# Linear attention's stages given out two slices later, and the modulations' sums ordered behind the scores' last step on VectorE

## The chip, the cores and the metric

The kernel runs on one core of one Trainium2 chip. The metric is the device time of one launch, in microseconds (us). The kernel before took 630.38 us, the median of three runs (629.6, 630.38, 630.89). Smaller is better.

## The reference

It is one layer of a diffusion backbone: 256 latent tokens (with 256 context tokens beside them) of width 1024, modulated by a conditioning vector, mixed by three branches in parallel, merged, and sent through a mixture of 16 experts. Cut to what the change touches:

```
shift1, scale1, gate1, shift2, scale2, gate2 = split(silu(c) @ w_mod + b_mod, 6)
h = modulate(rms_norm(x), shift1, scale1)
proj = h @ w_in                       # keys, values, decays, queries, gates, branch gates
# linear attention (gla), chunks of 64 tokens, forwards and backwards:
q_dec = q * exp(cum); k_inv = k * exp(-cum)
att = where(mask, q_dec @ k_inv.T, 0)            # "scores"
o = att @ v + q_dec @ state                      # "values", and the part carried by the states
y_gla = rms_norm(o) * silu(out_gate)             # "normed"
m = sum(sigmoid(gate_b) * (y_b @ w_b) for b in (hyena, gla, attention))
x = x + gate1 * (m @ w_out)
x = x + gate2 * moe(modulate(rms_norm(x), shift2, scale2))
```

The vectors `scale2` and `shift2` (`sc2`, `sh2` in the kernel) are products of one vector with a 1024x1024 weight each, and are needed only by the experts' stage.

## The kernel before

Everything is one function, `tile_backbone_layer`. The weights of the projections come from memory as float32 tiles (`wf`, 1 MB each) on SyncE's DMA queue. ScalarE casts half a tile at a time to its high part (`whi`, L281) and VectorE subtracts to get its low part (`wlo`, L282); TensorE then does three products for each piece, high by high, high by low and low by high (`proj_tok`, L689 to L691, into banks `pj`; `proj_col`, L699 to L701, into banks `pc`). Both `whi` and `wlo` have three buffers each.

A quarter of such a tile is a *slice*, and `weight_slice` hands slices out in turn. They are numbered by `nslice`; the ones that matter here are 16 to 23 (output gates of linear attention, `og`), 24 to 31 and 32 to 39 (attention queries, `aq0`, `aq1`) and 40 to 47 (first branch gate, `br0`). Piece names carry the tile's place: `wlo_aq010` is the low part of half 0, tile 1, first two slices of `aq0` (its names begin aq0); `wlo_010` belongs to the first branch gate.

Behind the matmuls of each slice `slice_done` gives out whatever two lists, `stages` and `mods`, hold for that slice's number. Giving out means that the instructions are written into the program there; a scheduler with a cost model of its own then settles the order on each engine. `tc.issue_after(last_mm[0])` adds an order, on TensorE alone, behind the last matmul of the slice. VectorE's instructions from `mods` have no such order: the scheduler puts them where its model has room.

The stages of linear attention come for two halves of the tokens, t = 0 and 1:

- `gla_scores(t)`: the part carried by the states (L1065, banks `go`) and the scores (L1087, banks `ga`) on TensorE, then on VectorE two predicated copies that apply the mask (L1090) and an addition of the two directions (L1091), all in the tile `aka`.
- `gla_values(t)`: TensorE adds the scores' part to `go` (L1099); ScalarE squares; VectorE scales the sums of squares (`sg`, L1105) and GpSimd raises them to the power -0.5 (L233).
- `gla_normed(t)`: VectorE refines the root (L240 to L242) and scales and gates the outputs (`yg`, L1113, four instructions).
- `gla_transpose(t)`: TensorE transposes (`ygT`), ScalarE and VectorE split into two parts (L1122, L1123).

Other stages between them are the rotary turn of the queries (`rp_q`, L1145 to L1149), their transposes (`qTp`, `kTp` for the keys, all L275) and the powers for their norms (`qv`, L1210, on GpSimd again L233).

The modulations' sums are vector work: `mod_load` (L365) brings a quarter of a weight column block, 1 MB (`wm`), and two `mod_macc` add its two rows of 1024 to a running sum on VectorE (L377, `macc<-wm*csg+macc`). The sum of `sc2` has its own tile; that of `sh2` lies in the tile `gt`. `mod_sums` then sums over the partitions on TensorE (L290, `mc_sc`, `mc_sh`). Quarter 3 of `sc2` (`wm_sc23`) and quarter 1 of `sh2` (`wm_sh21`) use one after the other the same slot of memory, number 14, and the attention queries' tile `qT` takes that slot next. The list gives out these maccs at slices 27 to 30 and 40.

Of the kernel before, what the change touches and what calls it, by code (L numbers as in the profile page):

```python
# [16 lines left out]
ALU = mybir.AluOpType  # L17
# [138 lines left out]
def tile_backbone_layer(ctx: ExitStack, tc: tile.TileContext, I: dict, out: bass.AP):  # L156
    nc = tc.nc
    V, S, T, G, SP = nc.vector, nc.scalar, nc.tensor, nc.gpsimd, nc.sync
# [24 lines left out]
    def slot(i, shape, nm, dtype=F32):  # L183
        return big.tile(shape, dtype, tag=f"s{i}", bufs=1, name=nm)
# [32 lines left out]
    def mbank(nm):  # L217
        return psM.tile([P, 512], F32, tag="mm", name=nm)
# [402 lines left out]
    for k4 in range(4):  # L621
# [4 lines left out]
                    op=ALU.add)  # L626
# [38 lines left out]
                modulated(0, step)  # L665


    stages, mods, nslice, last_mm = {}, {}, [-16], [None]

    def slice_done():  # L670

        with tc.issue_after(last_mm[0]):
            for f, *a in stages.pop(nslice[0], []) + mods.pop(nslice[0], []):
                f(*a)
        nslice[0] += 1

    def proj_tok(n, nm, streams, hook=None):
# [47 lines left out]
    for u in (2, 0, 1):  # L725
# [4 lines left out]
        for i in range(4):  # L730
            blk = u * 4 + i
            src = bk[i // 2][:, (i % 2) * NT:(i % 2 + 1) * NT]
            a = uc[u][:, i, :]
# [145 lines left out]
    for s, f, *a in ((None, hyena_time, 0),  # L879
# [20 lines left out]
        else:  # L900
            stages.setdefault(s, []).append((f, *a))
    bk = proj_tok(512, "kv1", (0, 1), slice_done)
    for r in range(2):
        for t in range(2):
            S.copy(gk[:, r, t, :], bk[r, t][:, 0:256])
            S.copy(gv[:, r, t, 0:256], bk[r, t][:, 256:512])
    bk = proj_tok(288, "kv2", (0, 1), slice_done)
    for r in range(2):
        for t in range(2):
# [142 lines left out]
    am, ygla = [], []  # L1052
# [3 lines left out]
    def gla_carried(t):  # L1056


        ob = obs[t] = [mbank(f"go{t}{hb}").rearrange("p (c v) -> p c v", c=4)[:, 0:2, :] for hb in range(2)]
        for cb in range(2):  # L1060
            for dr in range(2):
                for cp in range(2):
                    n = 2 * t + cp
                    for hb, hs in enumerate(half):
                        T.matmul(ob[hb][64 * cp:64 * cp + 64, cb, :], lhsT=qd[dr][hs, cb, n * 64:(n + 1) * 64],  # L1065
                                 rhs=St[hs, n, dr, cb, :], start=(cb == 0 and dr == 0), stop=False,
                                 skip_group_check=True)

    def gla_scores(t):
        gla_carried(t)  # L1070
        if t == 0:

            am.append(aka[:, 0:768].rearrange("p (d h c q) -> p d h c q", d=3, h=2, c=2))
            G.memset(am[0][:, 0:2], 0.0)

            am.append(gg[0][:, 512:640].rearrange("p (d q) -> p d q", d=2))
            for c in range(2):
                cs = slice(64 * c, 64 * c + 64)
                G.tensor_copy(am[1][cs], trg[cs, 0:2, cs])
            ygla.append(slot(15, [P, 2, 4, NT], "ygla", F32R))  # L1080
        ab = [mbank(f"ga{t}{hb}")[:, 0:256].rearrange("p (d c q) -> p d c q", d=2, c=2) for hb in range(2)]
        for dr in range(2):
            for cb in range(2):
                for cp in range(2):
                    n = slice(64 * (2 * t + cp), 64 * (2 * t + cp) + 64)
                    for hb, hs in enumerate(half):
                        T.matmul(ab[hb][64 * cp:64 * cp + 64, dr, cb, :], lhsT=ki[dr][hs, cb, n], rhs=qd[dr][hs, cb, n],  # L1087
                                 start=True, stop=True, skip_group_check=True)
        for hb in range(2):
            V.copy_predicated(am[0][:, 0:2, hb], am[1][:, :, None, :].bitcast(U32).to_broadcast([P, 2, 2, 64]), ab[hb])  # L1090
        V.tensor_tensor(am[0][:, 2], am[0][:, 0], am[0][:, 1], op=ALU.add)  # L1091

    def gla_values(t):
        ob = obs[t]
# [140 lines left out]
    for s, f in ((0, (decay_weights,)),  # L1235
                (0, (decay_inputs,)),
                (1, (decay_exp, 0)),
                (1, (decay_exp, 1)),
                (1, (decay_exp, 2)),
                (1, (decay_exp, 3)),  # L1240
                (5, (decay_log,)),
                (6, (context_keys, 0)),
                (7, (context_keys, 1)),
                (8, (decayed_keys, 0)),
                (8, (context_state,)),
                (9, (end_keys, 0)),
                (9, (end_keys, 1)),
                (10, (decayed_keys, 1)),
                (11, (key_norms,)),
                (13, (rope_tables,)),  # L1250
                (13, (key_rope, 0)),
                (14, (chunk_states, (0, 1))),
                (16, (key_rope, 1)),
                (17, (chunk_states, (3, 2))),
                (18, (key_transpose, 0)),
                (19, (key_rope, 2)),
                (19, (key_transpose, 1)),
                (21, (gla_scores, 0)),
                (23, (key_rope, 3)),
                (24, (gla_values, 0)),  # L1260
                (24, (key_transpose, 3)),
                (26, (gla_scores, 1)),
                (26, (gla_normed, 0)),
                (28, (gla_transpose, 0)),
                (27, (key_transpose, 2)),
                (30, (gla_values, 1)),
                (32, (gla_normed, 1)),
                (34, (gla_transpose, 1)),
                (33, (query_transpose, 0, 1)),
                (36, (query_transpose, 0, 0)),  # L1270
                (43, (query_transpose, 1, 0)),
                (43, (query_transpose, 1, 1))):
        stages.setdefault(s, []).append(f)
    aka = slot(16, [P, 2048], "aka")
    ak = aka[:, 1024:2048].rearrange("p (i d) -> p i d", i=4)
    av = slot(9, [P, 2, 4, 256], "av", F32R)
    bk = proj_tok(512, "kv0", (0, 1), slice_done)
    for r in range(2):
        for t in range(2):
# [680 lines left out]
```

## Time and profile before

| | before |
|---|---|
| median of 3 runs | 630.38 us |
| the profiled execution's own time | 629.4 us |
| its span in the trace | 627.6 us |
| TensorE busy | 598.1 us (95%) |
| VectorE busy | 363.2 us (58%) |
| ScalarE busy | 263.1 us (42%) |
| GpSimd busy | 34.0 us (5%) |
| mean granted clock of TensorE | 0.991 |

The span runs from the first to the last instruction; the execution's time has 1.8 us around it. The profiled execution was 0.98 us under the median. Linear attention's later stages and the attention queries lie between 180 and 260 us; the experts' stage, limited by TensorE, starts at about 408 us. Times in the views are us from the start of the span. "Idle before" an instruction is the time in which its engine did nothing just ahead of it, with what ended that.

### The profile page before, as it was taken

The numbers are of one execution on the slowest core, as the hardware profiler recorded it, in microseconds if no ns is written. First come the engines' busy times: TensorE is split into PE (matmuls) and PEld (weight loads), VectorE is DVE, ScalarE is ACT, GpSimd is POOL, SyncE is SP. The second block draws the span as 40 slices with busy tenths as digits, with TensorE's granted clock in tenths as the row PEclk, the third lists the DMA queues.
The fourth block names the chain that finished last, engine by engine and source line by source line (L and its number), as shares of the span: only waits on it lengthen the run. The fifth ranks groups of instructions, "written<-read, shape, count | busy, mean of one in ns | idle before, by whom it ended". The sixth has DMA issues, their size and how long they took to land.

```text
span 627.6 us, 9837 instructions
## 1 busy us (share of the span) xinstructions
PE 598.1 (95%) x3907; PEld 424.6 (68%) x3907; DVE 363.2 (58%) x675; ACT 263.1 (42%) x485; POOL 34.0 (5%) x37
## 2 busy tenths in 40 slices
PE   4799999999998999999999999899999999999994
PEld 2339878788886789899999999653534434343332
DVE  6779979597588898979974485430412303212122
ACT  4747851447754667655634444430302202111012
POOL 1200400030100210000000000000000000000000
PEclk9999999999999999999999999989999999999997
DMA  8997722155655446795998689989999999999992
GB/s 259 390 346 251 235 71 68 67 168 181 256 202 174 175 142 225 266 324 181 386 350 308 240 291 324 333 301 338 410 409 409 409 409 409 408 410 409 409 388 86
DMA packets 60701, 179.12 MB, mean 285 GB/s; under 512 B 4644, under 2 KB 7396, under 8 KB 59368
## 3 DMA queue, kind: packets, MB, share of 16 engines
q1 hardware_dynamic: 60288, 177.66, 76.2%
q8 instruction: 33, 0.54, 0.3%
q0 software_dynamic: 192, 0.47, 0.2%
q10 hardware_dynamic: 168, 0.29, 0.1%
q14 instruction: 20, 0.16, 0.1%
HBM read 177.35 MB, written 1.05 MB: 284 GB/s over the span
## 4 chain that ended last, share of the span: by engine, by line
PE 82%; DVE 8%; DMA 4%; ACT 3%; issue 1%; POOL 1%; SPq 0%; ACTq 0%; POOLq 0%
PE gug L270 9%; PE guu L270 9%; PE y L270 9%; PE pc_br L699 4%; PE pc_br L701 4%; PE pc_br L700 4%; PE accm L270 3%; PE hgm L270 3%; PE pj_kv L689 2%; PE pj_kv L691 2%; PE pj_kv L690 2%; PE pc_hy L700 2%; PE pc_hy L701 2%; DMA wm_sh<-in_w_mod_dram 2%; PE pc_hy L699 2%; PE yb L1331 2%
## 5 line engine op out<-in xcount | busy, mean ns | idle before, releaser
L270 PE MATMUL gug<-mg,hgm 128*64 128x512 f32 x256 | 59.6, 597 | 0.0
L1802 DVE SCALAR_TENSOR_TENSOR y<-y,gsl,gt 128x256 f32<-128x256 f32 x32 | 15.0, 488 | 76.7 <-PE y L270 73.8
L270 PE MATMUL guu<-mu,hgm 128*64 128x512 f32 x256 | 56.7, 595 | 0.0
L270 PE MATMUL y<-md,hT 128*64 128x512 f32 x256 | 56.6, 593 | 0.0
L699 PE MATMUL pc_br<-hThi,whi 128*128 128x256 f32 x192 | 55.5, 289 | 0.0
L701 PE MATMUL pc_br<-hThi,wlo 128*128 128x256 f32 x192 | 54.3, 284 | 0.0
L700 PE MATMUL pc_br<-hTlo,whi 128*128 128x256 f32 x192 | 54.2, 282 | 0.0
L270 PEld LDWEIGHTS y<-md,hT 128*64 128x64 f32 x256 | 18.2, 137 | 36.1 <-issue 31.4
L281 ACT CAST wkm<-y 128x256 fp32r<-128x256 f32 x32 | 11.9, 373 | 72.1 <-DVE y L1802 71.5
L270 PEld LDWEIGHTS guu<-mu,hgm 128*64 128x64 f32 x256 | 17.7, 137 | 33.1 <-issue 30.3
L270 PEld LDWEIGHTS gug<-mg,hgm 128*64 128x64 f32 x256 | 17.6, 138 | 32.5 <-issue 31.8
L699 PEld LDWEIGHTS pc_br<-hThi,whi 128*128 128x128 f32 x192 | 36.6, 191 | 1.4 <-issue 0.8
L700 PEld LDWEIGHTS pc_br<-hTlo,whi 128*128 128x128 f32 x192 | 36.7, 191 | 0.5
L689 PE MATMUL pj_kv<-whi_kv,hThi 128*128 128x512 f32 (+1 forms) x96 | 36.6, 381 | 0.0
L701 PEld LDWEIGHTS pc_br<-hThi,wlo 128*128 128x128 f32 x192 | 36.6, 191 | 0.0
L281 ACT CAST whi<-wf 128x1024 fp32r<-128x1024 f32 x24 | 25.2, 1050 | 24.8 <-PE pc_br L700 13.1
L690 PE MATMUL pj_kv<-wlo_kv,hThi 128*128 128x512 f32 (+1 forms) x96 | 34.7, 362 | 0.0
L691 PE MATMUL pj_kv<-whi_kv,hTlo 128*128 128x512 f32 (+1 forms) x96 | 34.5, 360 | 0.0
L282 DVE TENSOR_TENSOR wlo<-wf,whi 128x1024 fp32r<-128x1024 f32 x24 | 29.2, 1218 | 9.0 <-ACT whi L281 9.0
L1879 ACT COPY hT<-hp 128x512 f32<-128x512 f32 x8 | 4.7, 586 | 71.0 <-PE hp L275 71.0
L1865 DVE TENSOR_TENSOR sg<-sg,guu 128x512 f32<-128x512 f32 x8 | 5.5, 687 | 48.7 <-PE guu L270 48.7
L700 PE MATMUL pc_hy<-hTlo,whi_hy 128*128 128x256 f32 x96 | 27.3, 287 | 0.5 <-DVE hTlo L656 0.5
(459 smaller groups left out, 1495.3 us busy)
## 6 DMA issues: line engine op xcount, KB each, us to landing
mg<-in_moe_w_gate_dram SPq DMA_DIRECT2D x64, 512.0 KB, 10.2
mu<-in_moe_w_up_dram SPq DMA_DIRECT2D x64, 512.0 KB, 10.2
md<-in_moe_w_down_dram SPq DMA_DIRECT2D x62, 512.0 KB, 10.2
wf<-in_w_in_dram SPq DMA_DIRECT2D x12, 1024.0 KB, 7.9
wm<-in_w_mod_dram SPq DMA_DIRECT2D x7, 1024.0 KB, 12.0
wf_hy<-in_w_in_dram SPq DMA_DIRECT2D x5, 1024.0 KB, 8.9
wf_kv<-in_w_in_dram SPq DMA_DIRECT2D x4, 1024.0 KB, 5.1
wm_sc<-in_w_mod_dram SPq DMA_DIRECT2D x4, 1024.0 KB, 6.1
```

The lines of the kernel that those rows point to most:

```text
L270: m = f(*a, **kw)
L281: S.copy(hi, src)
L282: last_lo[0] = V.tensor_tensor(lo, src, hi.bitcast(F32), op=ALU.subtract).ins
L689: T.matmul(o, lhsT=hi[:, k, tk], rhs=whi, start=(k == 0), stop=False)
L690: T.matmul(o, lhsT=hi[:, k, tk], rhs=wlo, start=False, stop=False)
L691: last_mm[0] = T.matmul(o, lhsT=lo[:, k, tk], rhs=whi, start=False, stop=(k == 7)).ins
L699: T.matmul(o, lhsT=hi, rhs=mv[0], start=(first and i % 2 == 0), stop=False, skip_group_check=True)
L700: T.matmul(o, lhsT=hi, rhs=mv[1], start=False, stop=False, skip_group_check=True)
L701: return T.matmul(o, lhsT=lo, rhs=mv[0], start=False, stop=last, skip_group_check=True)
L1331: T.matmul(yb[:, (h % 2) * NT:(h % 2 + 1) * NT], lhsT=av[:, i, n, kvh * P:(kvh + 1) * P], rhs=p[:, n, :], start=(n == m == 0), stop=(n == ...
L1802: V.scalar_tensor_tensor(yf, yf, gsl, gt2[:, c * 512 + f:c * 512 + f + 256], op0=ALU.mult, op1=ALU.mult)
L1865: V.tensor_tensor(sg.rearrange("s (j p) -> s j p", j=4), sg.rearrange("s (j p) -> s j p", j=4), ub.rearrange("s (p j) -> s j p", j=4), op= ...
```

## The change

Three edits. `slice_done` gives out the stages first and the modulations' instructions behind them, these under a second order: behind the instruction that `stage_dve` holds, if there is one. `gla_scores` puts its last VectorE instruction, the addition, into `stage_dve`, so every modulation instruction that is given out after a scores stage stands behind that stage's addition on VectorE. And the table moves most of linear attention's stages one or two slices later.

```
     def slice_done():
         with tc.issue_after(last_mm[0]):
-            for f, *a in stages.pop(nslice[0], []) + mods.pop(nslice[0], []):
+            for f, *a in stages.pop(nslice[0], []):
                 f(*a)
+
+            with tc.issue_after(stage_dve[0]) if stage_dve[0] else ExitStack():
+                for f, *a in mods.pop(nslice[0], []):
+                    f(*a)
         nslice[0] += 1
...
-        V.tensor_tensor(am[0][:, 2], am[0][:, 0], am[0][:, 1], op=ALU.add)
+        stage_dve[0] = V.tensor_tensor(am[0][:, 2], am[0][:, 0], am[0][:, 1], op=ALU.add).ins
...
-                (24, (gla_values, 0)),
+                (25, (gla_values, 0)),
...
-                (26, (gla_scores, 1)),
-                (26, (gla_normed, 0)),
-                (28, (gla_transpose, 0)),
+                (27, (gla_normed, 0)),
+                (29, (gla_transpose, 0)),
                 (27, (key_transpose, 2)),
-                (30, (gla_values, 1)),
+                (28, (gla_scores, 1)),
+                (32, (gla_values, 1)),
...
```

`gla_normed(1)` and `gla_transpose(1)` go from 32 and 34 to 34 and 36. Behind the new lines all line numbers are 4 higher.

The first place is VectorE at the scores of the first half. Here `ga00` and `ga01` are that half's scores, `aka` the tile that the addition closes, `gt2` the sum of `sh2`; the first piece is the kernel before, the second the changed one.

```order
239 L377 SCALAR_TENSOR_TENSOR gt2_71<-wm_sh20_1984,csg_67,gt2_71 128x1024
240 L282 TENSOR_TENSOR wlo_aq001_1866<-wf_aq00_1804,whi_aq001_1865 128x1024
241 L1090 COPY_PREDICATED aka_1350<-gg_1712,ga00_1838 128x2x128
242 L1090 COPY_PREDICATED aka_1350<-gg_1712,ga01_1839 128x2x128
243 L377 SCALAR_TENSOR_TENSOR gt2_71<-wm_sh21_2053,csg_67,gt2_71 128x1024
244 L1091 TENSOR_TENSOR aka_1350<-aka_1350 128x256
245 L377 SCALAR_TENSOR_TENSOR gt2_71<-wm_sh21_2053,csg_67,gt2_71 128x1024
```

```order
237 L282 TENSOR_TENSOR wlo_aq001_1866<-wf_aq00_1804,whi_aq001_1865 128x1024
238 L1094 COPY_PREDICATED aka_1350<-gg_1712,ga00_1838 128x2x128
239 L1094 COPY_PREDICATED aka_1350<-gg_1712,ga01_1839 128x2x128
240 L1095 TENSOR_TENSOR aka_1350<-aka_1350 128x256
241 L1237 SCALAR_TENSOR_TENSOR gg_1712<-th0_1879,pj_og00_1716 128x512
242 L1237 SCALAR_TENSOR_TENSOR gg_1712<-th1_1882,pj_og01_1717 128x512
```

Three sums of `sh2` stood before, between and behind the three steps of the scores; now the low part of a weight, the two copies and the addition follow each other.

The second place is VectorE at the scores of the second half (`ga10`, `ga11`), before and changed; `kT` is the keys' transposed tile and `ygla` the split output of the first half.

```order
258 L282 TENSOR_TENSOR wlo_aq011_1987<-wf_aq01_1915,whi_aq011_1986 128x1024
259 L1090 COPY_PREDICATED aka_1350<-gg_1712,ga10_1953 128x2x128
260 L1090 COPY_PREDICATED aka_1350<-gg_1712,ga11_1954 128x2x128
261 L1091 TENSOR_TENSOR aka_1350<-aka_1350 128x256
262 L282 TENSOR_TENSOR wlo_aq100_2019<-wf_aq10_2016,whi_aq100_2018 128x1024
263 L282 TENSOR_TENSOR kT_1348<-kTp2_1996,kT_1348 128x2x128
264 L1123 SCALAR_TENSOR_TENSOR ygla_1837<-ygT0_2008,pk_65,ygla_1837 128x4x128
265 L282 TENSOR_TENSOR wlo_aq101_2062<-wf_aq10_2016,whi_aq101_2061 128x1024
266 L377 SCALAR_TENSOR_TENSOR gt2_71<-wm_sh22_2057,csg_67,gt2_71 128x1024
```

```order
254 L282 TENSOR_TENSOR wlo_aq100_2012<-wf_aq10_2009,whi_aq100_2011 128x1024
255 L282 TENSOR_TENSOR kT_1348<-kTp2_1957,kT_1348 128x2x128
256 L1094 COPY_PREDICATED aka_1350<-gg_1712,ga10_1987 128x2x128
257 L1094 COPY_PREDICATED aka_1350<-gg_1712,ga11_1988 128x2x128
258 L1095 TENSOR_TENSOR aka_1350<-aka_1350 128x256
259 L377 SCALAR_TENSOR_TENSOR macc_sc2_1213<-wm_sc23_1927,csg_67,macc_sc2_1213 128x1024
260 L377 SCALAR_TENSOR_TENSOR gt2_71<-wm_sh20_1935,csg_67,gt2_71 128x1024
261 L1127 SCALAR_TENSOR_TENSOR ygla_1837<-ygT0_2021,pk_65,ygla_1837 128x4x128
262 L377 SCALAR_TENSOR_TENSOR macc_sc2_1213<-wm_sc23_1927,csg_67,macc_sc2_1213 128x1024
263 L282 TENSOR_TENSOR wlo_aq101_2045<-wf_aq10_2009,whi_aq101_2044 128x1024
```

The low part `wlo_aq100` and the keys' copy now stand ahead of the scores' steps, and behind the addition come the two sums of `sc23`, which stood some sixty rows earlier (rows 199 and 201 of the kernel before), and the first sum of `sh20` (row 239 before). The rest of `sh2` follows in the changed program at rows 276 to 301, two each of `sh21`, `sh22` and `sh23`; the other product of `sh20`, the first of its sum, is ScalarE's (L375) in both kernels.

The third place is TensorE in the first branch gate, at the first use of the low part with number 2282 (`wlo_010`), before and changed; 2448 and 2449 are the banks of the same gate's second half.

```order
1046 L701 MATMUL pc_br_2262<-hThi_377,wlo_2200 128x256
1047 L275 MATMUL qTp_2337<-tri,rp_q_2233 128x128 x4
1048 L699 MATMUL pc_br_2261<-hThi_377,whi_2281 128x256
1049 L700 MATMUL pc_br_2261<-hTlo_378,whi_2281 128x256
1050 L699 MATMUL pc_br_2262<-hThi_377,whi_2281 128x256
1051 L700 MATMUL pc_br_2262<-hTlo_378,whi_2281 128x256
1052 L701 MATMUL pc_br_2261<-hThi_377,wlo_2282 128x256
1053 L699 MATMUL pc_br_2261<-hThi_377,whi_2281 128x256
```

```order
1051 L703 MATMUL pc_br_2262<-hThi_377,whi_2281 128x256
1052 L704 MATMUL pc_br_2262<-hTlo_378,whi_2281 128x256
1053 L703 MATMUL pc_br_2448<-hThi_377,whi_2377 128x256
1054 L704 MATMUL pc_br_2448<-hTlo_378,whi_2377 128x256
1055 L703 MATMUL pc_br_2449<-hThi_377,whi_2377 128x256
1056 L704 MATMUL pc_br_2449<-hTlo_378,whi_2377 128x256
1057 L275 MATMUL qTp_2337<-tri,rp_q_2233 128x128 x4
1058 L705 MATMUL pc_br_2261<-hThi_377,wlo_2282 128x256
```

Four matmuls of the gate's second half, which need only a high part, now stand ahead of the first matmul on `wlo_010`.

On TensorE the scores of the second half now come 12 projection matmuls and one transpose of keys later, its values from the last part of `aq0` into the first of `aq1`, and the eight column sums of `sh2` (L290) stand together, where before attention's products split them into five and three. On GpSimd the power of the first queries (`qv`, 128x8) now stands ahead of that of the second half's `sg` (128x4). On SyncE's queue the load of `wm_sh21` moves from behind the first tile of `aq0` to behind the first tile of the branch gate, seven issues later.

## Rows read from the trace of the kernel before

**Rows 1.** the profile page, part 1: busy us of each engine

```profile
PE 598.1 (95%) x3907; PEld 424.6 (68%) x3907; DVE 363.2 (58%) x675; ACT 263.1 (42%) x485; POOL 34.0 (5%) x37
```

**Rows 2.** waits of TensorE: line waited for, total us, times, longest us

```profile
PE go L1099 <- DVE aka L1091: 1.0, 1, 1.0
...
PE ga L1087 <- DVE yg L1113: 0.9, 1, 0.9
...
PE qTp L275 <- DVE rs_y L242: 0.5, 1, 0.5
```

**Rows 3.** VectorE's timeline: start us, us, engine, line, operation, tiles

```profile
191.46 1.27 DVE L377 SCALAR_TENSOR_TENSOR gt<-wm_sh,csg,gt 128x1024 f32<-128x1024 f32 x1
192.65 0.41 DVE L1091 TENSOR_TENSOR aka<-aka 128x256 f32<-128x256 f32 x1
```

**Rows 4.** TensorE's timeline, 194 to 200 us; idle before, and its releaser, in brackets

```profile
194.39 0.47 PE L689 MATMUL pj_aq<-whi_aq,hThi 128*128 128x512 f32 x1
...
197.33 1.10 PE L1065 MATMUL go<-St,qd 64*64 64x128 f32 x32
199.31 0.95 PE L1087 MATMUL ga<-qd,EK 64*64 64x64 f32 x32 [0.87 <-DVE yg L1113]
```

**Rows 5.** VectorE's timeline, 197 to 231 us

```profile
197.79 0.16 DVE L240 TENSOR_TENSOR rs_t<-rs_y 128x4 f32<-128x4 f32 x1 [0.80 <-POOL rs_y L233]
...
200.56 0.77 DVE L1090 COPY_PREDICATED aka<-gg,ga 128x256 f32<-128x256 uint32 x2
201.36 0.42 DVE L1091 TENSOR_TENSOR aka<-aka 128x256 f32<-128x256 f32 x1
...
204.12 0.41 DVE L282 TENSOR_TENSOR kT<-kTp,kT 128x256 fp32r<-128x256 f32 x1
...
229.46 1.22 DVE L282 TENSOR_TENSOR wlo<-wf,whi 128x1024 fp32r<-128x1024 f32 x1
```

**Rows 6.** one stretch by engine: us; busy (instructions); clock, DMA share, GB/s

```profile
201.78:230.67 28.89, 28.35 (x183) 23.50 (x181) 24.83 (x48) 19.57 (x59) 5.08 (x3) 1.00 0.52 182
```

**Rows 7.** TensorE's timeline at the column sums and at wlo_010's first use

```profile
222.25 1.10 PE L290 MATMUL mc_sc<-macc_sc,tri 128*32 128x128 f32 x16
...
231.06 0.28 PE L700 MATMUL pc_br<-hTlo,whi 128*128 128x256 f32 x1
231.18 0.28 PE L701 MATMUL pc_br<-hThi,wlo 128*128 128x256 f32 x1
...
255.38 1.07 PE L290 MATMUL mc_sh<-gt,tri 128*32 128x128 f32 x10
...
257.88 0.63 PE L290 MATMUL mc_sh<-gt,tri 128*32 128x128 f32 x6
```

**Rows 8.** GpSimd's timeline: the powers

```profile
196.75 1.01 POOL L233 TENSOR_TENSOR rs_y<-sg,mhalf 128x4 f32<-128x4 f32 x1 [26.25 <-DVE sg L1105]
209.78 2.03 POOL L233 TENSOR_TENSOR rs_y<-sg,mhalf 128x4 f32<-128x4 f32 x1 [12.02 <-DVE sg L1105]
215.46 2.08 POOL L233 TENSOR_TENSOR rs_y<-qv,mhalf 128x8 f32<-128x8 f32 x1 [3.65 <-DVE rs_t L241]
229.69 3.08 POOL L233 TENSOR_TENSOR rs_y<-qv,mhalf 128x8 f32<-128x8 f32 x1 [12.15 <-DVE qv L1210]
```

**Rows 9.** line L365 on SyncE's queue: times from issue to landing

```profile
DMA to landing us min/median/max: 4.7/6.1/8.1
```

**Rows 10.** TensorE's timeline ahead of the experts

```profile
406.19 0.38 PE L1691 MATMUL rk<-mask,tri 128*128 128x32 f32 x2 [2.23 <-DVE mask L1683]
...
407.61 0.69 PE L270 MATMUL hgm<-Om,x1hi 128*128 128x256 f32 x2 [0.83 <-DVE Om L1732]
```

**Rows 11.** stretches of 2 us behind it, columns as in group 6

```profile
408.00:410.00 2.00, 1.91 (x9) 1.70 (x10) 1.77 (x3) 0.00 (x0) 0.00 (x0) 0.61 1.00 373
410.00:412.00 2.00, 2.00 (x10) 1.66 (x11) 0.97 (x3) 0.87 (x2) 0.00 (x0) 0.53 0.99 397
412.00:414.00 2.00, 2.00 (x11) 0.71 (x8) 1.31 (x6) 0.57 (x3) 0.00 (x0) 1.00 0.17 61
```

More of the change, by code (lines that the diff above doesn't have):

```diff
@@ L665, in tile_backbone_layer @@
                 modulated(0, step)
-    stages, mods, nslice, last_mm = {}, {}, [-16], [None]
+    stages, mods, nslice, last_mm, stage_dve = {}, {}, [-16], [None], [None]
     def slice_done():
         with tc.issue_after(last_mm[0]):
-            for f, *a in stages.pop(nslice[0], []) + mods.pop(nslice[0], []):
+            for f, *a in stages.pop(nslice[0], []):
                 f(*a)
+            with tc.issue_after(stage_dve[0]) if stage_dve[0] else ExitStack():
+                for f, *a in mods.pop(nslice[0], []):
+                    f(*a)
         nslice[0] += 1
@@ L1259, in tile_backbone_layer @@
                 (23, (key_rope, 3)),
-                (24, (gla_values, 0)),
+                (25, (gla_values, 0)),
                 (24, (key_transpose, 3)),
-                (26, (gla_scores, 1)),
-                (26, (gla_normed, 0)),
-                (28, (gla_transpose, 0)),
+                (27, (gla_normed, 0)),
+                (29, (gla_transpose, 0)),
                 (27, (key_transpose, 2)),
-                (30, (gla_values, 1)),
-                (32, (gla_normed, 1)),
-                (34, (gla_transpose, 1)),
+                (28, (gla_scores, 1)),
+                (32, (gla_values, 1)),
+                (34, (gla_normed, 1)),
+                (36, (gla_transpose, 1)),
                 (33, (query_transpose, 0, 1)),
```

## The prediction

> **What bounds the kernel now.** I read the page first, then TensorE's waits, then the timelines of the two engines between 190 and 260 us, last the stretches. The page has TensorE busy for 598.1 us of the span of 627.6 [rows 1], so a gain can only come from the rest, or from matmuls that follow each other better. TensorE's waits show how much of that rest linear attention holds: its values wait 1.0 for VectorE's addition of the scores, its second scores 0.9 for the gated outputs `yg`, and one transpose of queries 0.5 [rows 2]. That is 2.4 us, and it is all that the change can take away there. Of the first wait 1.2 is a sum of `sh2`, which stands between the predicated copies and the addition: it starts at 191.46, the addition at 192.65 [rows 3]. But VectorE, at 58% over the span [rows 1], isn't loose here: between the end of the second addition and the end of `wlo_010`, a stretch of 28.89 us, it is busy for 24.83 [rows 6]. It has 4.06 us to give in that stretch.
>
> **What the change removes.** All three waits. For the first half the addition follows the copies directly, and TensorE has six projection matmuls and a transpose ahead of the values. The second scores come 12 matmuls later on TensorE, a good 2.9 us (194.39 to 197.33 [rows 4]), against a wait of 0.87 there. The third wait ended behind the same crowded VectorE; its transposes now come later. Sum: -2.4 us of waits, if nothing else is late.
>
> **What it moves.** The sums cost VectorE as much as before, 1.19 each (191.46 to 192.65 [rows 3]); only their place is new. Behind the second addition stand nine of them up to `wlo_010`, where four stood: two of `sc23`, one of `sh20` and two of `sh21` have come in. I follow VectorE to that point.
>
> - Start. The second `ga` ended at 199.31 + 0.95 = 200.26 [rows 4]. It loses the two waits ahead of it (1.0 + 0.87 = 1.86, unrounded) and gets the 12 matmuls with the switch to them (2.94): 201.34. Copies and addition take from 200.56 to 201.36 + 0.42 = 201.78 [rows 5], that is 1.22. So the addition ends at 202.6, against 201.78.
> - Work. 24.83 [rows 6] plus 5 x 1.19 = 5.95, less `wlo_aq100` and the keys' copy, which now stand ahead of the addition (1.2 as `wlo_010`, and 0.41 [rows 5]; 1.6 together): 29.2 us.
> - Idle. Of 4.06 before, nearly all goes, since the extra sums fill the time in which VectorE was ahead of the others. It can't be under 0. From above I take 0.7, the one gap of the kind that ended on a slower engine in rows here (0.80 <- GpSimd [rows 5]), less what the extra work hides; I use 0.35.
> - End of `wlo_010`: 202.6 + 29.2 + 0.35 = 232.15.
>
> TensorE first used `wlo_010` at 231.18, half a microsecond after it was there (229.46 + 1.22 = 230.68 [rows 5, 7]): it did not wait. Now it arrives, without its 2.4 of waits and with four matmuls ahead at 0.12 each (231.06 to 231.18 [rows 7]; 0.48), at 231.18 - 2.4 + 0.48 = 229.26, and waits until 232.15: about 2.9 us. The stalls removed are collected again at one place. What is left of the sum: 232.15 - 231.18 = +1.0 at that matmul, -0.48 for the four matmuls that are done by then.
>
> Behind it I add one gain: the column sums of `sh2` stood in two pieces, 1.07 and 0.63, and stand in one now, as those of `sc2` did in 1.10 [rows 7]. The difference is 0.6; since the last matmul of each piece overlaps what follows, I take 0.5. Other groups on TensorE (`ygT`, `qTp`) also get new neighbours; the same 0.6, either way, bounds them, and I take 0.
>
> Sum: +1.0 - 0.5 - 0.5 = 0.0 us.
>
> **What I cost at nothing.** The first half's `gla_normed` and `gla_transpose`, one slice later each: their readers are branch products far behind. The later end of `sc2`'s sum: its column sums stand at 222.25 [rows 7], and `sc23`'s second sum ends four VectorE instructions of at most 1.2 behind 202.6, by 207.4. That end also frees slot 14, and only then can `wm_sh21` be issued. It lands 4.7, 6.1 or 8.1 us later (least, median, most [rows 9]): 212.1, 213.5 or 215.5. VectorE reaches its first sum of `sh21` thirteen instructions later: three `wlo` at 1.2 and eight of the rotary turn, between the keys' copy's 0.41 [rows 5] for half their number and some 0.7 for those of double width (an estimate from it), so 7 to 8 us, 214.4 to 215.4. At the median the cover is 1 us; at the worst landing 1 us is lost. SyncE's queue holds other loads behind that issue, the branch gate's third and later tiles; they are wanted more than 10 us later.
>
> GpSimd's two powers change places: the one for `qv` now runs first, and the gated outputs of the second half need the other. From `qv`'s scaling to the first reader of `sg`'s power VectorE has two `wlo`, a sum, a last rotary step and a scaling, 4.2 us with the above durations; the two powers took 2.08 and 2.03 [rows 8], so 4.1. The cover is just enough. A power has also taken 1.01 and 3.08 [rows 8]. One at 3.08 costs 1.0, two cost 2.0, and as VectorE has no idle time left there, TensorE pays it. Bounds 0 and 2.0, and I take 0, by the two rows that are nearest in place.
>
> **The rivals.**
>
> *Faster: the waits go for good.* VectorE would have to have `wlo_010` when TensorE comes, at 229.26. Then -2.4 - 0.5 = -2.9: 627.5 against the median. For it: only one of nine sums is wanted soon. Against: the order on VectorE is fixed, and 29.2 us of work behind 202.6 can't end before 231.8. What I can see is a part of it: no idle (-0.35), scores some 0.3 sooner, neighbours that help (-0.6), about -1.3: 629.1.
>
> *Slower: the clock.* The collected wait of 2.9 us at one place costs more than itself if TensorE's clock falls. Ahead of the experts it was idle for 2.23, did a few small matmuls, and was idle again for 0.83 [rows 10]; the granted clock then showed 0.61 and 0.53 for 2 us each, and 1.00 again [rows 11]; behind linear attention's waits of 1.0 and 0.9 it was 1.00 [rows 2, 6]. The loss would be 2 x 0.39 + 2 x 0.47 = 1.7 us: 632.1. It decides from a wait about as long as that 2.23; against it, matmuls on high parts break mine up.
> [...]
>
> *Slower: GpSimd.* Its power took 1.01 where VectorE stood idle for 0.80 until it ended, and 2.03 to 3.08 in the stretch where VectorE had work [rows 5, 8]. In the changed kernel VectorE has no gap there, and two powers stand one behind the other: 1.0 to 2.0 us, 631.4 to 632.4.
> [...]
>
> *The change does less than it says* would be a scores' step that is still interrupted; the order on VectorE excludes it.
>
> **How the numbers follow.** The profiled execution took 629.4 us (span 627.6 and 1.8 around it), 0.98 under the median. With 0.0 the own time stays 629.4 and the median 630.4. What a measurement tells from no change is 0.2%, 1.26 us. Chances: the sum as worked out, with costs at their middle, 0.58; the gain, in part or whole, 0.16; the clock 0.13; GpSimd 0.13. Half of the last lies over 631.6, and a twentieth of the first goes there by a late `wm_sh21` or new neighbours; so slower 0.13 + 0.07 + 0.04 = 0.24, faster 0.16, same 0.60. The likeliest case's own range is 629.4 to 631.5 (idle 0 to 0.7, neighbours 0.6 either way, load 0 to 1). The range reaches to the clock's 632.1 above, and to the partial gain's 629.1 and a little below: 628.8 to 632.2.
>
> **What would show it.** In the changed profile: no wait of the values for the addition, nor of `ga` for `yg`; VectorE without gaps from about 202 to 232, over 98% busy; a new wait of TensorE for `wlo` (L282) of 2 to 3 us in the first branch gate, near 230; two sums of `sc` behind 202 us, and `wm_sh21` issued near 207. A clock under 1.00 between 228 and 236 is the second rival; a gap on VectorE ended by GpSimd the third. I am wrong if the wait for `wlo_010` is under 1 us, or if new waits stand in other places than the branch gate.

## The result: 0.5% slower

The changed kernel takes 632.77 us (median of 7 runs) against 630.16 (7 runs); the ratio is 1.0052, 95% interval 1.0032 to 1.0072. In a second comparison it was 631.99 against 629.40, ratio 1.0036, 1.0017 to 1.0055. (A ratio and its interval are estimated from all runs and need not be the quotient of the medians.) The predicted 630.4 was wrong, and the time lies above its range; so does 1.0036 of the 630.38 that it started from, 632.7. What the second rival said would happen did: behind TensorE's new wait of 1.70 us its granted clock was 0.50 in a stretch of 2 us.

The profiled execution took 632.19 us (span 630.3). It ran 0.7 us ahead of the one of before until the first scores, so I compare a stretch that both share: from the first half's carried scores to attention's last product. These are its first and last row on TensorE, of before:

```profile
186.25 1.10 PE L1065 MATMUL go<-St,qd 64*64 64x128 f32 x32
...
324.44 0.28 PE L1331 MATMUL yb<-pThi,av 128*128 128x256 f32 x1
```

and of the changed kernel:

```profile
185.54 1.10 PE L1069 MATMUL go<-St,qd 64*64 64x128 f32 x32
...
327.35 0.28 PE L1335 MATMUL yb<-pThi,av 128*128 128x256 f32 x1
```

The stretch has grown from 138.19 to 141.81, by 3.6 us; everything behind it takes the same time within 0.3. TensorE's waits in the changed kernel (line waited for, total, times, longest):

```profile
PE rk L1695 <- DVE mask L1687: 2.2, 1, 2.2
PE pc_br L705 <- DVE wlo L282: 2.2, 2, 1.7
...
PE mc_sh2c L296 <- ACT mc_sh2r L293: 0.9, 1, 0.9
...
PE pc_br L703 <- ACT whi L281: 0.5, 1, 0.5
```

The three waits of [rows 2] are gone; no line of them is left. In their place stand 2.2 for `wlo` (0.46 at `wlo_001`, 1.70 at `wlo_010`), 0.54 for the high part in between, 0.94 at the second step of `sh2`'s column sums, and 0.10 at the second `ga`. Together 3.74 for 2.40: waits alone make +1.3. Of the other 2.3 the clock makes 1.7, as the next rows show. The wait of 0.54 ended on ScalarE's cast of the high part, which had itself waited for TensorE's matmuls on an older one:

```profile
228.34 1.05 ACT L281 CAST whi<-wf 128x1024 fp32r<-128x1024 f32 x1 [1.05 <-PE pc_br L704]
```

The stretches around the new waits, with the columns of [rows 6]:

```profile
228.00:230.00 2.00, 1.46 (x11) 1.06 (x9) 1.67 (x3) 1.62 (x3) 0.00 (x0) 1.00 0.00 0
230.00:232.00 2.00, 0.88 (x6) 0.64 (x6) 2.00 (x5) 1.66 (x9) 0.47 (x1) 1.00 0.00 0
232.00:234.00 2.00, 1.43 (x9) 1.43 (x10) 2.00 (x4) 0.00 (x0) 2.00 (x1) 0.80 0.00 0
234.00:236.00 2.00, 2.00 (x8) 1.80 (x7) 2.00 (x4) 1.42 (x3) 0.01 (x1) 0.50 0.09 20
236.00:238.00 2.00, 2.00 (x16) 1.91 (x15) 1.87 (x4) 0.17 (x1) 0.00 (x0) 0.85 0.92 297
```

TensorE is busy for 1.46 and 0.88 of two stretches of 2 us, and behind them the granted clock is 0.80, 0.50 and 0.85, where it was 1.00 before. That is 2 x (0.20 + 0.50 + 0.15) = 1.7 us of clock. Its timeline shows what that does:

```profile
229.45 0.39 PE L703 MATMUL pc_br<-hThi,whi 128*128 128x256 f32 x1 [0.54 <-ACT whi L281]
...
230.28 0.60 PE L275 MATMUL qTp<-tri,rp_q 128*128 128x128 f32 x4
232.57 0.39 PE L705 MATMUL pc_br<-hThi,wlo 128*128 128x256 f32 x1 [1.70 <-DVE wlo L282]
...
233.31 1.05 PE L275 MATMUL qTp<-tri,rp_q 128*128 128x128 f32 x4
...
234.81 1.48 PE L1307 MATMUL sc<-kT,qT 128*128 128x512 f32 x3
...
255.61 0.86 PE L1307 MATMUL sc<-kT,qT 128*128 128x512 f32 x3
```

Four transposes took 0.60 at 230.28 and 1.05 at 233.31, and three score products 1.48 at 234.81; three such products took 0.86 at 255.61, where the clock was 1.00. Another 0.35 stand ahead of the fall, at a clock of 1.00: behind the wait of 0.54 four matmuls took 0.83 from start to start (229.45 to 230.28), at 0.12 each as in [rows 7] it would be 0.48. No row here says why.

VectorE does nearly what was worked out. Its rows from the second addition on, and the stretch up to the end of `wlo_010`:

```profile
201.46 0.42 DVE L1095 TENSOR_TENSOR aka<-aka 128x256 f32<-128x256 f32 x1
201.80 1.28 DVE L377 SCALAR_TENSOR_TENSOR macc_sc<-wm_sc,csg,macc_sc 128x1024 f32<-128x1024 f32 x1
...
213.64 1.32 DVE L377 SCALAR_TENSOR_TENSOR gt<-wm_sh,csg,gt 128x1024 f32<-128x1024 f32 x1 [0.20 <-DMA wm_sh<-in_w_mod_dram]
...
224.80 0.75 DVE L1127 SCALAR_TENSOR_TENSOR ygla<-ygT,pk,ygla 128x512 fp32r<-128x512 f32 x1 [0.70 <-ACT ygla L1126]
...
229.91 0.69 DVE L1149 TENSOR_TENSOR rp_q<-qs,ropet 128x512 f32<-128x512 f32 x1 [0.33 <-ACT qs L1199]
...
231.30 1.22 DVE L282 TENSOR_TENSOR wlo<-wf,whi 128x1024 fp32r<-128x1024 f32 x1
```

```profile
201.80:232.52 30.72, 28.08 (x177) 22.80 (x175) 29.36 (x51) 19.65 (x58) 5.11 (x3) 1.00 0.58 205
```

The addition ends at 201.88 (in before's times 0.7 later, 202.6; predicted 202.6), and the next instruction starts at 201.80. VectorE is busy for 29.36 us (predicted 29.2) of 30.72. The idle time is 1.36, where I took 0.35: 0.70 and 0.33 for ScalarE, 0.20 for the load of `wm_sh21`.

### The profile page after: what moved, and what is told of

Same layout as the page of the kernel before. It is cut to its first block, busy times and chain, and to the rows that moved or that the text cites. A ratio compares the mean times of both kernels' runs of the same rounds, so it can differ in the third digit from the quotient of the medians.

```text
span 630.3 us, 9835 instructions
## 1 busy us (share of the span) xinstructions
PE 599.3 (95%) x3907; PEld 426.6 (68%) x3907; DVE 363.2 (58%) x675; ACT 263.0 (42%) x485; POOL 33.6 (5%) x37
## 3 DMA queue, kind: packets, MB, share of 16 engines
HBM read 177.35 MB, written 1.05 MB: 283 GB/s over the span
## 4 chain that ended last, share of the span: by engine, by line
PE 78%; DVE 8%; DMA 6%; ACT 5%; issue 1%; POOL 1%; SPq 0%; ACTq 0%; DVEq 0%
PE gug L270 9%; PE guu L270 9%; PE y L270 9%; PE pc_br L705 3%; PE pc_br L703 3%; PE pc_br L704 3%; PE accm L270 3%; PE hgm L270 3%; PE pj_kv L693 2%; PE pj_kv L695 2%; PE pj_kv L694 2%; PE pc_hy L704 2%; DMA wm_sh<-in_w_mod_dram 2%; PE pc_hy L705 2%; PE pc_hy L703 2%; PE sc L1307 2%
```

## The experiments

Each was compared with the kernel before on its own chip. The stretch is the one above, read from TensorE's timeline of each profile, and its waits are the sum of the gaps that timeline shows there.

| kernel | median us | before | ratio, 95% interval | stretch | waits | stretch less waits | clock, 200 to 250 us |
|---|---|---|---|---|---|---|---|
| before | 630.16 | | | 138.2 | 2.4 | 135.8 | 1.00 |
| changed | 632.77 | 630.16 | 1.0052, 1.0032 to 1.0072 | 141.8 | 3.7 | 138.1 | 0.97 |
| changed, again | 631.99 | 629.40 | 1.0036, 1.0017 to 1.0055 | 141.3 | 3.5 | 137.9 | 0.97 |
| extra matmuls in the wait | 632.14 | 629.21 | 1.0040, 1.0025 to 1.0055 | 141.1 | 3.3 | 137.8, of it 1.8 extra | 1.00 |
| `sh23` late | 628.55 | 629.21 | 0.9989, 0.9971 to 1.0006 | 137.3 | 1.6 | 135.8 | 1.00 |
| table alone | 631.95 | 629.21 | 1.0032, 1.0013 to 1.0050 | 141.4 | 3.2 | 138.2 | 0.97 |
| order alone | 631.08 | 629.21 | 1.0032, 1.0015 to 1.0049 | 139.6 | 3.7 | 135.9 | 1.00 |
| `sh22`, `sh23` late | 627.33 | 629.40 | 0.9973, 0.9963 to 0.9982 | 137.2 | 1.3 | 135.9 | 1.00 |
| the same, values at 31 | 627.50 | 629.40 | 0.9970, 0.9960 to 0.9980 | 136.0 | 0.3 | 135.7 | 1.00 |
| the same, router filled | 626.96 | 629.40 | 0.9963, 0.9949 to 0.9978 | 136.4 | 0.6 | 135.8 | 1.00 |
| the same, router filled twice | 626.41 | 629.96 | 0.9947, 0.9935 to 0.9960 | 136.1 | 0.3 | 135.8 | 1.00 |
| changed, values at 31 | 632.21 | 629.96 | 1.0035, 1.0020 to 1.0050 | 141.3 | 3.2 | 138.1 | 0.97 |

The seventh column is the main result. Without its waits (and the extra matmuls, 136.0) the stretch takes 135.7 to 136.0 us in every profile whose clock stays at 1.00, and 137.9 to 138.2 in every one whose clock falls. Against before's 135.8 a profile with a fall is 2.1 to 2.4 us longer beside its waits, whichever wait is ahead of it. The clock's own rows give 1.7 of that; the rest is not in them. All this is read from one profile of each kernel. The medians don't show the clock by itself: extra matmuls and order alone, with the clock at 1.00 in their profiles, are as slow (1.0040, 1.0032) as the kernels whose clock falls.

**Extra matmuls in the wait.** Does the clock's fall cost, or only the wait? (Here and at the router the extra matmuls are written over several lines, and their argument `skip_group_check=True` is left out.)

```
     def query_transpose(u, t):
         b = mbank(f"qTp{u}{t}")
+        if (u, t) == (1, 0):
+            for _ in range(8):
+                T.matmul(b, lhsT=hT[0][0][:, 0, 0:P], rhs=hT[0][0][:, 0:2, :], start=True, stop=True)
```

> The changed kernel with eight extra 128x512 matmuls on TensorE into the bank of the queries' transpose qTp10, ahead of the transposes that overwrite them: work without use, about 8 x 0.23 = 1.8 us, that TensorE does while it would wait for wlo_010 in any case (its waits there were 0.54 and 1.70). VectorE's, ScalarE's, GpSimd's and SyncE's orders are the changed kernel's. Theory A (the clock): the wait's end, near 232.5, stays, but the granted clock stays at 1.00 from 232 to 238, where it showed 0.80, 0.50 and 0.85 in stretches of 2 us; the 2 x (0.20 + 0.50 + 0.15) = 1.7 us come back: 1.7 us faster than the changed kernel, about 631.1 where that is 632.8. Rival B (the loss is new waits alone, the clock's fall costs nothing that counts): no difference, 632.8, or up to 1.8 slower.

The clock stayed at 1.00. The stretches are those in which it was 0.80, 0.50 and 0.85, and the one before:

```profile
230.00:232.00 2.00, 2.00 (x16) 1.84 (x15) 1.67 (x5) 1.89 (x10) 0.00 (x0) 1.00 0.00 0
232.00:234.00 2.00, 1.07 (x10) 0.87 (x9) 2.00 (x4) 0.59 (x1) 1.73 (x1) 1.00 0.00 0
234.00:236.00 2.00, 2.00 (x17) 1.87 (x16) 2.00 (x4) 0.90 (x2) 0.74 (x1) 1.00 0.03 8
236.00:238.00 2.00, 2.00 (x19) 2.00 (x19) 2.00 (x5) 1.57 (x4) 0.00 (x0) 1.00 0.63 160
```

But the stretch is only 0.7 shorter than in the changed kernel's first profile, and 0.2 shorter than in its second, not 1.7. The rest went to something else: VectorE now waited 0.90 for GpSimd, as it did not in the changed kernel's first profile, but did in its second (below), and `wlo_001` came 0.65 later (a wait of 1.11 for 0.46). From the first matmul on `wlo_010` (233.30 here, 232.57 there) to the last product it is 93.43 against 94.78, 1.35 less, although the column sums waited 0.2 longer (1.15). Without that wait it is 92.28 here, and 93.84 and 93.60 in the changed kernel's two profiles: the fall costs 1.3 to 1.6 there, near the 1.7 of the clock's rows. So the extra matmuls kept the clock up, and the clock's price is shown in the stretch alone; the total, 632.14 at a ratio of 1.0040, misses the gain of 1.7 that was expected and doesn't separate the two kernels.

**`sh23` late.** Take work out of VectorE's full stretch.

```
-                  (40, mod_macc, "sh2", 3, 0),
-                  (40, mod_macc, "sh2", 3, 1),
+                  (46, mod_macc, "sh2", 3, 0),
+                  (47, mod_macc, "sh2", 3, 1),
```

> The changed kernel with the two sums of sh23 given out at slices 46 and 47 instead of 40: they leave VectorE's full stretch ahead of wlo_010 (2 x 1.2 = 2.4 us). Theory A (VectorE's stretch sets the wait, and the wait the clock): the waits of 0.54 and 1.70 go (2.2), the clock stays at 1.00 (1.7): 3.9 us faster than the changed kernel, 628.9 where that is 632.8, and about 1.3 faster than before. Rival B (waits alone): 2.2 faster, 630.6. Rival C (the sums are only late somewhere else): a wait of over 1 us appears behind 235, and the time is 631 or more.

As theory A says in the main: no wait for `wlo_010`, clock at 1.00, stretch 4.5 shorter than the changed kernel's (predicted 3.9). Two sums of 1.2 us, given out six and seven slices later, take away the whole loss. Against before it is not separated (0.9971 to 1.0006); a wait of 1.16 for `wlo_001` is left. That wait, and the stretch of 10 us around `wlo_010`, in which TensorE was never idle:

```profile
223.17 0.39 PE L705 MATMUL pc_br<-hThi,wlo 128*128 128x256 f32 x1 [1.16 <-DVE wlo L282]
```

```profile
228.00:238.00 10.00, 10.00 (x82) 9.78 (x81) 9.86 (x19) 7.29 (x22) 3.68 (x1) 1.00 0.32 107
```

**Table alone** (without `stage_dve`):

```
-            with tc.issue_after(stage_dve[0]) if stage_dve[0] else ExitStack():
+            with ExitStack():
```

> The table's shift alone, without the order behind the scores' addition. Theory A: sums stand between the scores' steps again and one wait of some 0.9 at ga stays, no wait of over 1 us in the branch gate, clock 1.00 there: between 629.5 and 631.2 where before is 630.2. Rival B: the table's shift by itself makes the kernel slower (work is given out too late): the changed kernel's 632.8.

A miss: 631.95 at a ratio of 1.0032, above the 631.2 (1.0016 of 630.2) that I allowed. Rival B's sign came true, the table by itself makes the kernel slower, but by another way than work that is given out too late. I hadn't seen that the sums, free again, would hold up `yg` by more than 0.9. TensorE's waits, and the stretches behind them:

```profile
202.31 0.99 PE L1069 MATMUL go<-St,qd 64*64 64x128 f32 x27 [1.60 <-DVE yg L1117]
...
203.94 0.93 PE L1091 MATMUL ga<-qd,EK 64*64 64x64 f32 x30 [0.54 <-DVE kT L282]
```

```profile
200.00:202.00 2.00, 0.71 (x4) 0.19 (x2) 1.20 (x6) 1.13 (x2) 0.58 (x1) 1.00 0.59 138
202.00:204.00 2.00, 1.16 (x36) 0.95 (x38) 1.88 (x4) 0.00 (x0) 0.00 (x0) 1.00 1.03 392
204.00:206.00 2.00, 2.00 (x33) 1.69 (x34) 1.07 (x3) 0.00 (x0) 0.00 (x0) 0.56 0.06 12
206.00:208.00 2.00, 2.00 (x10) 1.51 (x8) 0.13 (x1) 0.24 (x1) 0.00 (x0) 0.59 0.87 289
```

Two waits, 1.60 and 0.54, one behind the other, and the clock at 0.56 and 0.59. It is the pair of the changed kernel (0.54 and 1.70) at another place, 30 us earlier, with the same price in clock, 2 x (0.44 + 0.41) = 1.7.

**Order alone** (the table of before, with `stage_dve`; the diff is the table's part of the change, reversed):

> The order behind the scores' addition alone, with the table of before. Theory A: the extra sums behind the second addition make TensorE wait, but about two slices earlier, for ygT and for wlo of aq1, some 3 us in several pieces, against 2.4 removed. If pieces of under 2 us with work between them leave the clock at 1.00, 630 to 631; if one piece of about 1.7 is enough, a clock under 1.00 behind it and 1.7 more, 632 to 633. Rival B (the table's shift is what costs): 630 or less.

The first case of theory A: four waits between 214 and 221 us, and the clock at 1.00.

```profile
214.47 0.63 PE L275 MATMUL qTp<-tri,rp_q 128*128 128x128 f32 x4 [0.55 <-DVE rp_q L1153]
...
217.36 0.33 PE L275 MATMUL ygT<-tri,yg 128*128 128x128 f32 x1 [0.17 <-DVE yg L1117]
...
218.82 0.33 PE L275 MATMUL ygT<-tri,yg 128*128 128x128 f32 x1 [0.69 <-DVE yg L1117]
220.54 0.50 PE L694 MATMUL pj_aq<-wlo_aq,hThi 128*128 128x512 f32 x1 [1.40 <-DVE wlo_aq L282]
```

Its waits sum to as much as the changed kernel's (3.7 each, here 2.8 in these four), and its stretch is 2.2 shorter: 1.7 of that is the clock. Why it stayed up here is open. The last two waits (0.69 and 1.40) make nearly as much as the changed kernel's two, and lie closer, with 0.3 us of work between them for 1.4. The kernel's runs reach from 628.99 to 633.75, so that in other executions the clock may have fallen; one was profiled. Each half of the change is slower than before; by their intervals neither can be told from the whole.

**The changed kernel again.**

> The changed kernel again, beside the next three on the same chip. Both theories: 1.003 to 1.007 of the kernel before, that is 2 to 4.4 us slower; in its profile the stretch from the first carried scores (L1069) to attention's last product (L1335) is 141.8 us against 138.2 before, if the wait at wlo_010 and the clock's fall repeat.

The wait and the fall repeat (1.70; 0.93 over 225 to 250 us). Three things differ from its first profile. There the column sums of `sh2` waited 0.94, here not at all; the wait for `wlo_001` is 1.11 for 0.46; and here VectorE waited for GpSimd. GpSimd's powers in the first profile, and in this one:

```profile
210.58 3.15 POOL L233 TENSOR_TENSOR rs_y<-qv,mhalf 128x8 f32<-128x8 f32 x1 [14.02 <-DVE qv L1214]
213.69 1.00 POOL L233 TENSOR_TENSOR rs_y<-sg,mhalf 128x4 f32<-128x4 f32 x1
```

```profile
210.80 3.15 POOL L233 TENSOR_TENSOR rs_y<-qv,mhalf 128x8 f32<-128x8 f32 x1 [14.02 <-DVE qv L1214]
213.92 1.81 POOL L233 TENSOR_TENSOR rs_y<-sg,mhalf 128x4 f32<-128x4 f32 x1
```

```profile
215.77 0.16 DVE L240 TENSOR_TENSOR rs_t<-rs_y 128x4 f32<-128x4 f32 x1 [0.90 <-POOL rs_y L233]
```

The one for `qv` takes 3.15 in both, where I had counted 2.08; behind it that for `sg` takes 1.00 or 1.81. It was 1.00 where VectorE had stood idle for 0.20 just ahead of it, from 213.44 to 213.64, for the late `wm_sh21`; then VectorE was busy for the whole of that 1.00. That the gap made the difference is argued, not tried. The 0.9 on VectorE in the second profile is the third rival at work.

**`sh22` and `sh23` late.** All four sums behind the branch gate's first half:

```
-                  (30, mod_macc, "sh2", 2, 0),
-                  (30, mod_macc, "sh2", 2, 1),
+                  (44, mod_macc, "sh2", 2, 0),
+                  (45, mod_macc, "sh2", 2, 1),
...
-                  (40, mod_macc, "sh2", 3, 0),
-                  (40, mod_macc, "sh2", 3, 1),
+                  (48, mod_macc, "sh2", 3, 0),
+                  (49, mod_macc, "sh2", 3, 1),
```

> The changed kernel with the sums of sh22 given out at slices 44 and 45 and those of sh23 at 48 and 49: all four sums leave the stretch ahead of wlo_010 (4.8 us of VectorE). Theory A (VectorE's stretch and behind it the clock): no wait for wlo_010, clock at 1.00 from 200 to 400, and since VectorE now has slack behind GpSimd's powers, the wait of 1.16 for wlo_001 that the version with only sh23 moved still had shrinks to under 0.5: the stretch from L1069 to the last L1335 at 136.5 to 137, 1.2 to 1.7 less than before's 138.2. Rival C (late sums only wait elsewhere): 138 or more, with a new wait at the column sums of sh2 near 255.

627.33, ratio 0.9973: faster than before, with an interval clear of 1. The stretch, 137.2, lies a little over theory A's 137. No wait over 0.6 is left; those for `wlo_001` and `wlo_010` are gone.

**The same, values at 31.**

```
-                (32, (gla_values, 1)),
+                (31, (gla_values, 1)),
```

> As the kernel before this one, and the second half's values given out at slice 31 instead of 32: GpSimd's power for sg then stands ahead of that for qv, as in the kernel before. Theory D (GpSimd's order costs what VectorE can't hide): no idle time of VectorE that ends on GpSimd, and the stretch 0.3 to 0.7 shorter than with sh22 and sh23 late alone, about 136.2. Rival: with slack on VectorE the order of the powers costs nothing; same as that kernel.

GpSimd has the old order again, 1.45 and then 2.08, and VectorE no longer waits for it. The stretch is 1.2 shorter in the profile (more than the 0.3 to 0.7 expected) and almost without waits, but the medians are the same, 627.33 and 627.50. Against before, both kernels give some of their gain back at the experts. Stretches of 4 us there, from 404 and from 408, first with values at 31, then the kernel before it:

```profile
404.00:408.00 4.00, 2.78 (x13) 2.60 (x14) 3.83 (x10) 0.10 (x1) 0.00 (x0) 0.63 1.00 359
408.00:412.00 4.00, 4.00 (x15) 2.33 (x16) 2.21 (x9) 1.44 (x4) 0.00 (x0) 0.52 0.69 275
```

```profile
404.00:408.00 4.00, 1.87 (x7) 1.71 (x7) 3.44 (x15) 1.02 (x2) 0.00 (x0) 0.65 0.98 365
408.00:412.00 4.00, 4.00 (x17) 3.15 (x17) 2.45 (x6) 1.13 (x2) 0.00 (x0) 0.50 0.82 325
```

Before, the clock's rows gave 1.7 us there [rows 11]; here they give 4 x 0.37 + 4 x 0.48 = 3.4, and 4 x 0.35 + 4 x 0.50 = 3.4 for the kernel before this one. As both have it, it doesn't say why their medians are the same, which stays open. Both versions' profiled executions were the slowest of their runs (629.0 and 628.23), so even against before it is not shown for the medians.

**Router filled**, once and twice: matmuls without use in the waits of [rows 10], ten calls and then six more (20 and 12 instructions in the trace, 2.40 and 1.58 us).

```
-    rk = gbank("rk")
+    rk = gbank("rk")
+    for _ in range(10):
+        T.matmul(rk[:, 0:P], lhsT=ones, rhs=lt, start=True, stop=True)
...
             b = ybank(f"hg{pf}{q}{k2}")
+            for _ in range(6 if k2 == 0 and not wk else 0):     # second version only
+                queued(T.matmul, b[:, 0:P], lhsT=ones, rhs=lt, start=True, stop=True)
```

> As the kernel before this one, with ten extra 128x128 matmuls on TensorE into the router's bank rk, ahead of the products that overwrite it: about 2 us of work without use in the wait of 2.23 that every kernel here has near 406, behind which the clock falls to about half for some 4 us. Theory A (a wait of about 2 us or more with little work around it lowers the clock, and work without use prevents it): clock at 1.00 from 408 to 416, 1.7 us of clock back at the experts' start, and 1 to 1.7 us less in total. Rival (the experts' weights come no sooner, so the time is given back): clock at 1.00 there, time within 0.5 us of the kernel without the extra matmuls. If the clock falls all the same, theory A lacks something.

> As the kernel with ten extra matmuls ahead of the router, and six more 128x128 matmuls behind the router's products, into the bank that the first gathering product overwrites: they fill the wait of 1.44 that was left there and behind which the clock fell all the same (0.71, 0.50, 0.94 in stretches of 2 us). Theory A: with both waits under 0.5 the clock stays at 1.00 from 400 to 416; against the kernel without extra matmuls 1.0 to 1.7 us less, about 0.994 to 0.995 of the kernel before. Rival (given back to the experts' weights or to VectorE): clock 1.00 and under 0.5 us less.

With the first wait filled the clock fell all the same, behind the second, which had grown to 1.44:

```profile
405.50 0.69 PE L270 MATMUL hgm<-Om,x1hi 128*128 128x256 f32 x2 [1.44 <-DVE Om L1736]
```

With both filled it did not fall. The first two lines are the kernel filled once, the last two that filled twice:

```profile
404.00:408.00 4.00, 2.46 (x13) 2.08 (x13) 3.52 (x11) 0.71 (x3) 0.00 (x0) 0.85 0.94 358
408.00:412.00 4.00, 4.00 (x18) 2.05 (x18) 1.92 (x6) 0.72 (x2) 0.00 (x0) 0.72 0.48 197
```

```profile
404.00:408.00 4.00, 3.89 (x29) 3.32 (x28) 3.86 (x12) 0.35 (x3) 0.00 (x0) 1.00 0.97 357
408.00:412.00 4.00, 4.00 (x25) 2.26 (x26) 2.12 (x7) 1.27 (x3) 0.00 (x0) 1.00 0.74 278
```

From attention's last product to the last matmul it is 295.1 us, against 296.8 without extra matmuls and 296.1 before. This is the fastest version of all, 0.9947 of before (0.9935 to 0.9960); without the extra matmuls it was 0.9970 (0.9960 to 0.9980), so some 1.4 us are theirs, by intervals that just touch, on two chips and with 5 and 8 runs.

**The changed kernel, values at 31.** Is GpSimd's order the cause of the loss?

> The changed kernel with the second half's values given out at slice 31 instead of 32, so that GpSimd's power for sg stands ahead of that for qv, as before the change; no sum is moved. Theory A (the sums in VectorE's full stretch are the cause): TensorE still waits 1.5 us or more for wlo_010, the clock falls behind it, and the time is the changed kernel's, 1.003 to 1.005 of before. Theory D (GpSimd's powers behind each other are the cause): VectorE's idle time of 0.9 ends, the wait goes under 1, the clock stays at 1.00, 1.000 or less.

Theory A: VectorE's wait for GpSimd is gone, TensorE's for `wlo_010` is 1.67, the clock is 0.93 over 225 to 250 us, and the time is the changed kernel's. GpSimd's order isn't what makes the change slower.

## Why the prediction was wrong

- *The three waits go.* Right, 2.40.
- *VectorE's full stretch collects them at `wlo_010`.* Right in mechanism and place. The size, 2.7 in three pieces (0.46, 0.54, 1.70) where 2.9 in one was worked out, is in part luck. `wlo_010` was ready at 232.52, 233.2 in before's times, 1.1 later than the 232.15 worked out, for 1.0 more idle time on VectorE. TensorE came at 230.87, 231.6 in before's times, 2.3 later than 229.26: 1.1 of that are the waits of 0.10, 0.46 and 0.54, and some 0.6 are the column sums of `sc2` (next point). And 0.54 ended on ScalarE, not on VectorE.
- *The column sums of `sh2` give 0.5.* Wrong. They stand in one piece (1.10), but those of `sc2`, whole before [rows 7], now stand in two, which I had not looked for:

```profile
223.16 0.62 PE L290 MATMUL mc_sc<-macc_sc,tri 128*32 128x128 f32 x2
...
223.97 1.09 PE L290 MATMUL mc_sc<-macc_sc,tri 128*32 128x128 f32 x14
```

  TensorE's time on L290 over the stretch is 3.90 before and 3.91 after. And the second step of `sh2`'s sums, a place that I hadn't named, could wait for ScalarE: 0.94 in the first profile, nothing in the second one of the same kernel. ScalarE's copy stands there behind a cast that waits for its weight tile (1.05 at 260.66, and 0.32 in the second profile); that this tile's place on SyncE's queue decides it is argued, not tried.
- *The clock stays.* This is the step that failed. I had it as a rival at 0.13, with a wait "about as long as that 2.23" as its point, and thought that matmuls on high parts would break mine up. Waits of 0.54 and 1.70 with four matmuls and four transposes between them were enough. Its price was what the rival had, 1.7 by the clock's rows. The sum put it at nothing, and that was the fault, not its size. The stretch less its waits is longer by more, 2.1 to 2.4; of the difference 0.35 stands behind the wait of 0.54, and the rest has no row.
- *GpSimd hides.* Wrong by size: `qv`'s power took 3.15, not 2.08, and VectorE lost 0.9 in four of the five profiles that have this order with both halves of the change. By itself it decides nothing (values at 31). The rival took a power's length from what VectorE did beside it: 1.01 with VectorE idle for 0.80 of it, 2.03 with VectorE at work [rows 5, 8]. The 1.00 at 213.69, beside a VectorE that was busy throughout, does not fit that, and no run shows what sets the length.
- *The sum.* Predicted -2.4 + 2.9 - 0.5 = 0.0. Measured in the stretch -2.4 + 2.8 (with the 0.10 at `ga`) + 0.94 + 2.3 (1.7 of it the clock) = +3.6. Two sums behind it were off as well: a twentieth of 0.58 is 0.03, so slower had 0.23 and not 0.24; and 0.35, 0.6 and 1.0 on top of 630.4 make 632.3 for the likeliest case, not 631.5, over the 632.2 that the whole range went to.

## What to carry to other kernels

A sum of waits that came out even was not even on TensorE: the waits removed (1.0, 0.9 and 0.5) cost their length, while about the same time collected at one place also cost the clock, 1.7 us more by its rows. So where a change moves waits together, give the clock's price a weight in the sum, not beside it. Work between the waits was no safety by itself: the changed kernel had 1.4 us of it and its clock fell, order alone had 0.3 and in its profile kept 1.00. And look for what fills the waiting engine's queue without a date: two sums of 1.2 us that nobody wanted for 30 us made the difference between a loss of 0.4 to 0.5% and none.

## What the runs showed of the hardware

- Behind waits of 1.60 and 0.54 (table alone), and of 0.54 and 1.70 (changed), the granted clock was 0.50 to 0.59 in at least one whole stretch of 2 us, and behind a single 1.44 at the router (filled once) it was 0.50 in one. Behind 0.69 and 1.40 (order alone) it stayed at 1.00 in the one execution that was profiled. By these, length alone doesn't tell.
- Work without use on TensorE can pay: with sixteen matmul calls in two waits at the router the clock stayed at 1.00, and some 1.4 us came back, by intervals that just touch. In the branch gate the clock stayed at 1.00 with eight too, and the ratio, 1.0040, lay between the changed kernel's two, 1.0036 and 1.0052.
- The fall at the router took 1.7 us of clock in the kernel before and 3.4 in two others, with the same two waits there (2.2 and 0.8). A gain elsewhere in a kernel can be hidden by that difference of 1.7.
- A power over 128x4 elements on GpSimd took 1.00 (changed) to 2.03 us (before) in these profiles, one over 128x8 1.63 (`sh22`, `sh23` late, values at 31) to 3.68 (`sh23` late).
